# Two-layer hybrid encoder on one core: opening the next pair of heads while the one in front is still worked on, and moving attention's late products

## The chip, the cores and the metric

The kernel runs on one core of one Trainium2 chip, in one launch. The metric is the device time of that launch in microseconds (us). Five instruction queues matter: TensorE (PE, matrix products; its weight loads are listed apart as PEld), VectorE (DVE), ScalarE (ACT), GpSimd (POOL) and SyncE (SP), which issues most of the transfers. Every engine works through its own list of instructions in order, so an instruction that waits holds up all that stand behind it on that engine.

## The reference, cut to what matters

Each of two layers normalises the residual stream (1024 tokens by 1024 features), projects it with one matrix, feeds three kinds of heads, gates and projects their outputs and adds them to the stream; a norm of its own ends the program.

```python
def reference(x, positions, ...):
    for layer in range(DEPTH):                       # 2 layers
        h = rms_norm(x, norm_g[layer])
        cols = split_columns(h @ w_in[layer])
        y_gdn = gdn_branch(cols, ...)                # 6 heads, gated delta rule, both directions
        y_mla = mla_branch(cols, positions, ...)     # 6 heads, softmax attention with low-rank q and kv, rope
        y_rwkv = rwkv7_branch(cols, ...)             # 4 heads, RWKV-7 time mixing, both directions
        mix = jnp.concatenate([y_gdn.astype(F32), y_mla.astype(F32), y_rwkv.astype(F32)], axis=-1)
        mix = mix * jax.nn.silu(cols['gate'].astype(F32))
        x = x + mix.astype(x.dtype) @ w_out[layer]
    return rms_norm(x, final_norm_g)
```

The two recurrent kinds run a scan over the tokens, forwards and backwards. The GDN scan is written in chunks (a triangular solve inside each chunk, a state carried from chunk to chunk), and the kernel treats RWKV-7 in the same way.

## The kernel before, in words

**Two streams of work.** While the program is written out, a planner in Python decides the order of everything. One stream is the *scan stream*: first phase R (RWKV, 2 pairs of heads), then phase G (GDN, 3 pairs). Every pair is *opened* (its features loaded, normalised, transposed), its chunks are *prepared* (the products inside a chunk and the triangular inverse, L922 to L988), *stepped* through (16 steps that carry the state) and *closed* (both directions joined, transposed back by L839, gated into `mix`). The other is the *dense stream*: the input projection (27 tiles of 128 output columns), then the attention heads (MLA, 3 pairs by 2 halves of the tokens), into which the output projection of the RWKV heads (`out_part`) and the loading of output weights (`out_open`) are woven. What remains of the output projection comes after both.

**The rounds.** `chain` runs the scan stream in rounds. A round takes one piece from the scan thread and one from each preparation that is under way, and after each of them lets the dense stream advance by a share of `DENSE_R` or `DENSE_G`, in the planner's own microseconds. The dense generators yield such numbers after each group of instructions; `yield 0.0` gives way to the woven partner without counting, and `yield PAUSE` ends the dense stream's turn. The opening of a new pair is part of the first preparation of that pair (`nxt % nst == 0`); in the kernel before it starts only when no other preparation is under way, and `rwkv_open` waits besides (`GATE`) until the pair in front has delivered its `mix`. A scheduler then places the instructions on the engines, and `order()` ties the dense products on TensorE behind scan rows so that the two streams stay mixed as planned.

**The input projection** (`in_tiles`). A tile's weights arrive in `wf` (one buffer). `in_fetch` has two halves: the load and the column maximum `wc` on DVE (L529, L530); then a product with ones on TensorE that finds the maximum over partitions (`col_sum`, L509), a scale (DVE L510, L533, L534), and the split into two halves of f16, `wh` (ACT L537, L538) and `wl` (POOL L539). A tile has 48 products of 512 columns: for each of two halves of the tokens and eight blocks of the features the three products L378 to L380. The second half of the next tile's fetch is written into the middle of the present tile's products. `norm_T` normalises and transposes the input ahead of the first tile (64 transposes, L486). The evictions of the two halves (`post`) hand the tile on: a short convolution, a token shift, a gate, or the MLA latents (stored to DRAM).

**Attention** (`mla`). `latents` loads what the projection stored, squares it on ACT (L1512), sums over partitions by products with ones (L1523 to L1525), makes a reciprocal root on DVE (L397) and broadcasts it (L1544). `mla_q` projects the queries; their rotary part needs two more products (L1699, L1700), a combination on DVE (L1708) and a transfer that puts it beside the rest (L1715, `mq<-mr`). `mla_max` finds each query's maximum in a first pass of the scores (L1734, DVE L1735, L1739, transposed by L1744, moved by L1747 into `mnr`), `mla_main` computes scores (L1767 to L1769), exponentials (ACT L1771) and products with the values (L1778), `mla_side` is woven into it and holds the next queries and maxima, and `mla_tail` (L1810, two transfers through DRAM, L1824, L1829) normalises and gates.

**Scales of GDN** (`gdn_scales`). After the last gate column is projected, a chain of DVE and ACT work makes the decay factors; its products on TensorE begin with L795.

Of the kernel before, what the change touches and what calls it, by code (L numbers as in the profile page):

```python
# [222 lines left out]
DENSE_R = 0.85  # L223
DENSE_G = 1.05
LEAD = 4
GATE = "gate"
PAUSE = -1.0
# [6 lines left out]
class K:  # L234
# [307 lines left out]
    def in_tiles(self, l, tiles, xt, ss):  # L542
# [4 lines left out]
        w = next(f)  # L547
        yield from self.norm_T(l, xt, ss)
        hi, lo = self.h
        for i, (t, post, after) in enumerate(tiles):  # L550
# [4 lines left out]
            for nh in range(2):  # L555
                ps = self.A()
                sl = slice(512 * nh, 512 * nh + 512)
                for k in range(8):
                    ks = slice(128 * k, 128 * k + 128)
                    self.mm3(ps, [(wh[:, ks], wl[:, ks], hi[k][:, sl], lo[k][:, sl])], k == 0, k == 7)  # L560
                    yield 0.65
                    if nh and k == 2:
                        self.flush()
                    if not nh and k == 6 and i + 1 < len(tiles):
                        w = next(f)
                self.pending = post(nh, ps, sl, us) or self.pending
                yield 0.0
            if after:
                self.flush()
                after()  # L570
# [12 lines left out]
    def layer(self, l, xt, ss, last):  # L583
# [9 lines left out]
        with self.phase("R", 6, "right"):  # L593
            self.rwkv()
# [3 lines left out]
        with self.phase("G", 4, "right"):  # L598
            self.gdn()
# [10 lines left out]
    def dense_work(self, l, xt, ss):  # L610
# [16 lines left out]
        def scales():  # L627
            self.gdn_scales()

# [4 lines left out]
        for hp in range(3):  # L634
            tiles += [(8 + 3 * hp + j, self.conv_tile(hp, j), scales if hp == j == 2 else None) for j in range(3)]
# [124 lines left out]
    def gdn_scales(self):  # L760
# [31 lines left out]
        rows = scr[:, 528:784]  # L792
        ps = self.E()
# [367 lines left out]
    def chain(self, units, nst, ahead, early, stagger, dense, prep, step, close):  # L1161
# [48 lines left out]
        while S or ps or nxt < total:  # L1210
            if nxt < total and nxt <= done[0] + 1 + span and (not ps or ((nxt % nst or early) and len(ps) < span and ps[-1].at >= stagger)):
                ps.append(thread(preparation, nxt, nxt % 2))
                nxt += 1
# [34 lines left out]
    def rwkv_open(self, hp, w2):  # L1248
        nc = self.nc
        s = {"hp": hp, "w2": w2}  # L1250
        while hp and 5 + hp not in self.mix:
            yield GATE
# [192 lines left out]
    def rwkv_close(self, s):  # L1445
# [20 lines left out]
        sq = self.S("ysq")  # L1466
# [25 lines left out]
    def latents(self):  # L1492
# [9 lines left out]
        for nh in range(2):  # L1502
# [45 lines left out]

            for a in ((0, cq0, self.par("qg0"), 128, *c0), (0, t2, self.par("qg1"), 64, c1[0:64], c1[64:128]),
# [16 lines left out]
    def mla(self):  # L1566
# [3 lines left out]
        for pr, nh in units:  # L1570
            if pr == nh == 0:
                yield from self.weave(self.mla_first(), self.out_part(self.l))
# [33 lines left out]
    def mla_side(self, pr, nh):  # L1606
        if nh == 0:
            if pr == 0:
                yield from self.mla_q(pr, 1)
                for _ in range(4):  # L1610
                    yield 0.0
# [245 lines left out]
    def out_part(self, l):  # L1857
# [9 lines left out]
        for _ in range(6):  # L1867
            yield 0.0
# [106 lines left out]
```

## Time and profile before

| what | us |
|---|---|
| median of 3 runs | 2594.94 (2589.27 to 2595.14) |
| the profiled execution | 2594.93 |
| its span (first to last instruction) | 2593.1 |
| TensorE busy | 2274.3 (88%) |
| VectorE / ScalarE / GpSimd busy | 1681.8 / 1384.2 / 835.0 |
| granted TensorE clock, mean | 0.937 |

The stages of the first layer, from the timeline: the norm and its transposes up to 48, the first tiles of the projection alone up to 95, phase R from 95 to 600 (the steps of its two pairs from 150 to 312 and from 396 to 557), phase G from 600 to 1224 (steps of its three pairs from 617 to 792, 839 to 1009 and 1055 to 1222), the rest of the output projection up to 1307. The second layer repeats them: phase R from 1380 to 1880, phase G to 2500, output to 2593.

How to read the views that follow. A row of the waits gives the engine and line that waited, after the arrow what released it, then total us, how often, and the longest. A row of the windows gives a stretch of the span in us, its length, the busy time of TensorE (and, where more engines are listed, PE, PEld, DVE, ACT and POOL in this order), the mean granted clock as a share of full speed, the busy share of the DMA engines and GB/s. A row of the timeline gives the start, the duration, engine and line, output and inputs, and in brackets the idle time just before with its releaser. Durations of products on TensorE overlap, since they are pipelined.

### The profile page before, as it was taken

What the parts mean: (1) busy time and instruction counts of PE and PEld (TensorE: products, weight loads), DVE (VectorE), ACT (ScalarE), POOL (GpSimd) and SP (SyncE); (2) the same over time, 40 slices, a digit from 0 to 9 for tenths busy, and PEclk for the clock granted to TensorE, in tenths of its full rate; (3) what the DMA queues carried; (4) which work ended last, traced back from release to release, by engine and by line L of the source; (5) the groups of instructions that cost most, each with busy time, mean ns of one, the idle gap of its engine ahead of it and who ended that gap; (6) DMA issues with size and microseconds to landing.
All of it is one profiled execution on the core that took longest, in us unless ns stands there. A gap on an engine that the chain in (4) does not pass through costs nothing. (4 is left out here: it accounts for less than half of the span.)

```text
span 2593.1 us, 54912 instructions
## 1 busy us (share of the span) xinstructions
PE 2274.3 (88%) x21524; PEld 1391.3 (54%) x21524; DVE 1681.8 (65%) x3706; ACT 1384.2 (53%) x3077; POOL 835.0 (32%) x1079
## 2 busy tenths in 40 slices
PE   5999988898799889897989999898997998898978
PEld 3456555555565445554755555555555644455456
DVE  6566668845577775666245676777465777657655
ACT  5566656656445544554245665666463455455541
POOL 1223222323224535353012332232332256353510
PEclk9999999899889989898999989998997999898979
DMA  3122222223341111102212221222323411111131
GB/s 123 46 53 57 67 70 54 70 82 99 107 152 32 36 50 36 30 23 83 82 69 54 57 61 61 70 62 52 116 71 120 129 42 38 36 38 33 50 106 65
DMA packets 140338, 174.09 MB, mean 67 GB/s; under 512 B 37072, under 2 KB 95536, under 8 KB 140080
## 3 DMA queue, kind: packets, MB, share of 16 engines
q1 hardware_dynamic: 139936, 170.19, 21.7%
q8 instruction: 170, 2.79, 0.4%
q14 instruction: 88, 0.72, 0.1%
q0 software_dynamic: 144, 0.39, 0.1%
HBM read 106.88 MB, written 39.04 MB: 56 GB/s over the span
## 5 line engine op out<-in xcount | busy, mean ns | idle before, releaser
L378 PE MATMUL pa<-h,wh 128*128 128x512 f16 x864 | 335.1, 388 | 0.0
L379 PE MATMUL pa<-h,wh 128*128 128x512 f16 x864 | 334.3, 387 | 0.0
L380 PE MATMUL pa<-h,wl 128*128 128x512 f16 x864 | 333.3, 386 | 0.0
L948 DVE TENSOR_TENSOR z<-pb,c 128x256 f16<-128x256 f32 (+1 forms) x320 | 155.9, 487 | 149.5 <-PE pb L922 138.0
L926 ACT COPY bdz<-z 64x256 f16<-64x256 f16 (+1 forms) x384 | 172.8, 455 | 136.7 <-DVE z L948 112.2
L1773 POOL TENSOR_TENSOR md<-md,mp 128x512 f32<-128x512 f32 x144 | 188.5, 1313 | 133.3 <-ACT mp L1771 126.2
L539 POOL TENSOR_TENSOR wl<-wf,wh 128x512 f16<-128x512 f32 x108 | 127.6, 1196 | 282.6 <-ACT wh L538 274.9
L1778 PE MATMUL pa<-mp,mv 128*64 128x512 f32 x384 | 190.2, 634 | 0.0
L966 ACT CAST xT<-pe 128x512 f16<-128x512 f32 x256 | 150.8, 589 | 50.2 <-PE pe L965 49.3
L953 ACT CAST x<-pb 128x256 f16<-128x256 f32 (+1 forms) x320 | 134.8, 421 | 59.1 <-PE pb L922 58.0
L1735 DVE TENSOR_REDUCE mmx<-pa 128x1 f32<-128x512 f32 x192 | 131.3, 688 | 49.6 <-PE pa L1734 47.0
L1771 ACT ACTIVATE mp<-pa 128x512 f32<-128x512 f32 x192 | 114.5, 597 | 89.1 <-PE pa L1769 86.1
L927 DVE COPY bdz<-z 64x256 f16<-64x256 f16 (+1 forms) x384 | 150.5, 399 | 13.4 <-PE pe L958 0.9
L922 PEld LDWEIGHTS <-xT 128*128 128x128 f16 x1600 | 77.7, 99 | 106.3 <-issue 61.4
L1413 POOL TENSOR_TENSOR rs_e<-rs_z,rw_em 64x128 f32<-64x128 f32 x120 | 56.0, 482 | 239.6 <-DVE rs_z L1440 201.1
L922 PEld LDWEIGHTS <-bdgh 128*128 128x128 f16 x1920 | 89.3, 100 | 81.4 <-issue 43.5
L380 PEld LDWEIGHTS <-wl 128*128 128x128 f16 x864 | 85.6, 99 | 80.0 <-issue 8.3
L922 PE MATMUL pb<-z,xT 128*128 128x64 f16 x1600 | 108.9, 196 | 21.9 <-DVE z L948 20.0
L736 DVE SCALAR_TENSOR_TENSOR cacc<-raw,dv,cacc 128x512 f32<-128x512 f32 x144 | 120.5, 853 | 11.2 <-ACT cacc L730 9.5
L378 PEld LDWEIGHTS <-wh 128*128 128x128 f16 x864 | 90.1, 104 | 67.7 <-issue 9.6
L1734 PE MATMUL pa<-mk,mq 96*128 96x512 f32 (+1 forms) x192 | 93.4, 490 | 31.8 <-DMA mq<-mr 21.7
L379 PEld LDWEIGHTS <-wh 128*128 128x128 f16 x864 | 85.6, 99 | 57.8 <-issue 8.0
(462 smaller groups left out, 5683.1 us busy)
## 6 DMA issues: line engine op xcount, KB each, us to landing
wf<-in_w_in_dram SPq DMA_DIRECT2D x54, 512.0 KB
q_d<-cacc SPq DMA_DIRECT2D x18, 512.0 KB
rw_ka<-rw_kr SPq DMA_DIRECT2D x32, 256.0 KB
rw_ka<-rw_ak SPq DMA_DIRECT2D x64, 128.0 KB
gate_d<-gate SPq DMA_DIRECT2D x16, 512.0 KB
wof<-in_w_out_dram SPq DMA_DIRECT2D x16, 512.0 KB
xp_d<-mp SPq DMA_DIRECT2D x32, 256.0 KB
xo<-xp_d SPq DMA_DIRECT2D x16, 512.0 KB
```

Of the source, the lines that this page charges most:

```text
L378: self.did = nc.tensor.matmul(out, lhsT=lh, rhs=rh, start=(first and idx == 0), stop=False)
L379: self.did = nc.tensor.matmul(out, lhsT=lh, rhs=rl, start=False, stop=False)
L380: self.did = nc.tensor.matmul(out, lhsT=ll, rhs=rh, start=False, stop=(last and idx == n - 1))
L922: self.did = nc.tensor.matmul(ps[:, 64 * u:64 * u + 64], lhsT=st(lhsT, u), rhs=rhs(u), start=True, stop=True)
L926: nc.scalar.copy(zb[self.H[0], :, 0], t[self.H[0]])
L927: nc.vector.tensor_copy(zb[self.H[1], :, 1], t[self.H[1]])
L948: nc.vector.tensor_tensor(out=self.q8(z), in0=v(ps), in1=self.m8(self.c2(f"w{k}"), w), op=ALU.mult)
L953: nc.scalar.copy(f2(x), p1[:, :64 * nu])
L966: nc.scalar.copy(xn[:, g:g + 4].rearrange("p u h i -> p (u h i)"), p2)
L1735: nc.vector.tensor_reduce(out=mx[:, h, t:t + 1], in_=ps, axis=AX.X, op=ALU.max)
L1773: nc.gpsimd.tensor_tensor(out=acc[h], in0=prev[h] if t == 1 else acc[h], in1=pT, op=ALU.add)
L1778: self.did = nc.tensor.matmul(po[NR[h]], lhsT=vv[:, t, 2 * pr + h], rhs=pT[h], start=(t == 0), stop=(t == 7))
```

## The change

- The condition in `chain` loses its special case: a preparation that opens a new pair may start while the last preparation of the pair in front is under way. `rwkv_open` no longer waits for the `mix` of the pair in front. The phases get two more slots of scratch (6 to 8 and 4 to 6), and `rwkv_close` uses the tile `pbn` again in place of a slot of its own.
- `DENSE_R` goes from 0.85 to 1.0 and `DENSE_G` from 1.05 to 1.03.
- The second half of a fetch is written later: for the first tile after the ninth step of `norm_T` (before: ahead of all of it), for the others after the first group of the tile's second half (before: after the seventh group of its first half, ahead of that half's eviction).
- `gdn_scales` becomes a generator of the dense stream and pauses it for six turns ahead of L795.
- `latents` yields twice more ahead of its sums, in each half; at the start of attention both woven streams issue their first loads, and then pause for six turns.
- `mla_side` gives way eight times ahead of the second half's maxima, for each pair (before: four times, and for pair 0 only); `out_part` gives way once in place of six times.
- The scratch for descriptors of dynamic transfers becomes 8192 bytes.

```diff
-DENSE_R = 0.85
-DENSE_G = 1.05
+DENSE_R = 1.0
+DENSE_G = 1.03
...
         f = self.in_fetch(l, tiles[0][0])
         next(f)
-        w = next(f)
-        yield from self.norm_T(l, xt, ss)
+        for n, us in enumerate(self.norm_T(l, xt, ss)):
+            yield us
+            if n == 8:
+                w = next(f)
...
-                    if not nh and k == 6 and i + 1 < len(tiles):
+                    if nh and k == 0 and i + 1 < len(tiles):
                         w = next(f)
...
             if after:
                 self.flush()
-                after()
+                yield from after()
...
-        with self.phase("R", 6, "right"):
+        with self.phase("R", 8, "right"):
...
-        with self.phase("G", 4, "right"):
+        with self.phase("G", 6, "right"):
...
         rows = scr[:, 528:784]
+        for _ in range(6):
+            yield PAUSE
         ps = self.E()
...
-            if nxt < total and nxt <= done[0] + 1 + span and (not ps or ((nxt % nst or early) and len(ps) < span and ps[-1].at >= stagger)):
+            if nxt < total and nxt <= done[0] + 1 + span and (not ps or (len(ps) < span and ps[-1].at >= stagger)):
...
         s = {"hp": hp, "w2": w2}
-        while hp and 5 + hp not in self.mix:
-            yield GATE
...
-        sq = self.S("ysq")
+        sq = pbn
...
+            for _ in range(2):
+                yield 0.1
             for a in ((0, cq0, self.par("qg0"), 128, *c0), (0, t2, self.par("qg1"), 64, c1[0:64], c1[64:128]),
...
             if pr == nh == 0:
-                yield from self.weave(self.mla_first(), self.out_part(self.l))
+                first, part = self.mla_first(), self.out_part(self.l)
+                for g in (first, part):
+                    next(g)
+                for _ in range(6):
+                    yield PAUSE
+                yield from self.weave(first, part)
...
             if pr == 0:
                 yield from self.mla_q(pr, 1)
-                for _ in range(4):
-                    yield 0.0
+            for _ in range(8):
+                yield 0.0
             yield from self.mla_max(pr, 1)
...
-        for _ in range(6):
-            yield 0.0
+        yield 0.0
...
-    nc = _bacc.Bacc("TRN2", target_bir_lowering=False, num_devices=1)
+    nc = _bacc.Bacc("TRN2", target_bir_lowering=False, num_devices=1, dynamic_dma_scratch_size=8192)
```

Line numbers in the changed kernel differ by a few: one less up to the scales, one more in `chain`, the scans and their preparation (L839 becomes L840, L922 becomes L923), one less in the closing of RWKV and the latents, six more in attention (L1700 becomes L1706, L1734 becomes L1740, L1767 becomes L1773). How the change moves the rows of TensorE is seen at three places; a row has the line, the operation, output and inputs with their running numbers, and the width of the output.

TensorE at the first half of the latents in layer 0, where L1523 (in the changed kernel L1522) sums the squares in `mk`. Before, the rows just ahead are the scan's preparation:

```order
L958 LDWEIGHTS bdz_977_6574
L958 MATMUL pe_8005<-xs_1233_7908,bdz_977_6574 128x64
L1523 MATMUL pa_8021<-cst,mk_7962 128x1
L1524 MATMUL pa_8021<-cst,mk_7964 128x1
L1525 MATMUL pa_8021<-cst,mk_7966 128x1
```

and now:

```order
L978 LDWEIGHTS bdgl_979_6600
L978 MATMUL pb_8032<-x_1272_8014,bdgl_979_6600 128x64
L1522 MATMUL pa_8045<-cst,mk_7904 128x1
L378 MATMUL pa_8086<-wo_7920,mx_7910 128x512
L1523 MATMUL pa_8045<-cst,mk_7906 128x1
L379 MATMUL pa_8086<-wo_7921,mx_7910 128x512
L1524 MATMUL pa_8045<-cst,mk_7908 128x1
```

Products of `out_part` (`mx`, `wo`) now stand between the sums, and from the last product of the projection to the first sum there are 97 rows where there were 41.

TensorE at the second half's maxima of pair 1 in layer 0: the rotary products (L1699, L1700) end the queries, and the first L1734 with `mq_11370` is the first of these maxima; the earlier L1734 rows belong to the maxima of another half. Before, 44 rows lie from L1700 to it, the last of them the scan's outputs:

```order
L1699 MATMUL pa_11464<-c_7936,mw_1830_10387 128x512
L1700 MATMUL pa_11464<-c_7936,mw_1831_10388 128x512
L1734 MATMUL pa_11474<-mk_11226,mq_10401 128x512
...
L1128 MATMUL pc_11376<-gs_s_11442,gd_qg_10854 64x64
L1129 MATMUL pc_11376<-gs_u_11526,gd_pt_10873 64x64
L1734 MATMUL pa_11584<-mk_10841,mq_11370 128x512
```

and now 173:

```order
L1705 MATMUL pa_11614<-c_7878,mw_1861_10536 128x512
L1706 MATMUL pa_11614<-c_7878,mw_1862_10537 128x512
L1740 MATMUL pa_11624<-mk_11342,mq_10550 128x512
...
L923 LDWEIGHTS bdgh_978_6598
L923 MATMUL pb_11907<-i_79,bdgh_978_6598 128x64
L1740 MATMUL pa_11913<-mk_10982,mq_11531 128x512
```

Scan rows and the main part of attention have come in between.

TensorE at the end of layer 0: L1128 and L1129 (now L1129 and L1130) are the scan's last output products, L839 (now L840) transposes the closed pair, L378 with `mx` begins the rest of the output projection. Before:

```order
L1128 MATMUL pc_15085<-gs_s_15105,gd_qg_14708 64x64
L1129 MATMUL pc_15085<-gs_u_15126,gd_pt_14727 64x64
L839 MATMUL pe_15161<-cst,osum_12527 64x64 x16
L839 MATMUL pe_15179<-cst,osum_12527 64x64 x16
L378 MATMUL pa_15265<-mq_14357,mx_15224 128x512
```

and now:

```order
L1130 MATMUL pc_15026<-gs_u_15083,gd_pt_14573 64x64
L1775 MATMUL pa_15103<-mq_13537,mk_13384 128x512
L1784 MATMUL pa_14599<-mp_15048,mv_9164 64x512
L1784 MATMUL pa_14599<-mp_15069,mv_9164 64x512
L1784 MATMUL pa_14599<-mp_15091,mv_9164 64x512
L1784 MATMUL pa_14599<-mp_15107,mv_9164 64x512
L1816 MATMUL pa_15138<-md_14600,cst 64x512
L1816 MATMUL pa_15138<-md_14601,cst 64x512
L509 MATMUL pa_15203<-ngs_15201,cst 128x1
L840 MATMUL pe_15159<-cst,osum_12304 64x64 x16
L840 MATMUL pe_15177<-cst,osum_12304 64x64 x16
L378 MATMUL pa_15263<-mq_14690,mx_15222 128x512
```

The last products of attention stand behind the scan's last row, where before they stood ahead of it.

More of the change, by code (lines that the diff above doesn't have):

```diff
@@ L625, in plain @@
             return post
-        def scales():
-            self.gdn_scales()
         self.projected, self.pending = False, None
@@ L634, in dense_work @@
         for hp in range(3):
-            tiles += [(8 + 3 * hp + j, self.conv_tile(hp, j), scales if hp == j == 2 else None) for j in range(3)]
+            tiles += [(8 + 3 * hp + j, self.conv_tile(hp, j), self.gdn_scales if hp == j == 2 else None) for j in range(3)]
             if hp == 0:
```

## The prediction, made before the changed kernel ran

> **What bounds the kernel now.** The page's head and clock strip come first:
>
> ```profile
> span 2593.1 us, 54912 instructions
> PE 2274.3 (88%) x21524; PEld 1391.3 (54%) x21524; DVE 1681.8 (65%) x3706; ACT 1384.2 (53%) x3077; POOL 835.0 (32%) x1079
> PEclk9999999899889989898999989998997999898979
> ```
>
> TensorE works 88% of the span and the next engine 65%, and most slices are at or near full clock. Its busy time is no floor, though: several slices show 7 to 9 tenths of the clock, so some of the 2274.3 us is slow work. Next, who TensorE waited for (total, times, longest):
>
> ```profile
> PE pa L1734 <- DMA mq<-mr: 21.7, 4, 6.7
> PE pa L509 <- DVE wc L530: 20.0, 10, 5.0
> PE pe L958 <- DVE bdz L927: 20.0, 15, 2.4
> PE pa L1523 <- ACT mk L1512: 15.5, 2, 7.8
> PE pe L839 <- DVE osum L1152: 13.8, 2, 6.9
> PE pa L1544 <- DVE rq_y L397: 13.2, 4, 3.9
> PE pa L795 <- DVE scr L789: 7.2, 2, 3.6
> PE pa L1767 <- DMA mq<-mnr: 4.4, 6, 1.0
> ```
>
> Except for the many small waits of L958 (inside the scans), these are a few places per layer, each struck once or twice per layer. So I looked at each place by windows (length, PE busy, granted clock):
>
> ```profile
> core 0: us, PE busy (x), PEclk, DMA share, GB/s
> 502.00:513.00 11.00, 5.49 (x51) 0.53 0.14 24
> 676.00:697.00 21.00, 11.78 (x72) 0.51 0.48 152
> 710.00:728.00 18.00, 13.46 (x111) 0.53 0.30 95
> 935.00:953.00 18.00, 9.63 (x69) 0.53 0.32 103
> 1079.00:1100.00 21.00, 14.28 (x111) 0.51 0.12 33
> 1219.00:1243.00 24.00, 13.52 (x139) 0.50 0.23 68
> 1785.00:1797.00 12.00, 6.24 (x55) 0.57 0.13 22
> 1956.00:1977.00 21.00, 11.39 (x70) 0.51 0.50 154
> 1990.00:2008.00 18.00, 13.47 (x110) 0.53 0.29 97
> 2215.00:2233.00 18.00, 9.45 (x61) 0.53 0.33 101
> 2362.00:2377.00 15.00, 9.62 (x71) 0.54 0.11 28
> 2492.00:2517.00 25.00, 12.58 (x140) 0.52 0.23 62
> sum 222.00, PE 130.91; mean PE 10.91
> ```
>
> Six places, twice (layer 0, then layer 1): L795; the latents' first half; their second; the maxima of pair 1 (L1734); those of pair 2; the layer's end. Around each wait the clock stands near half, so a window costs its idle time and slow work besides. I take what a window could do at full clock as busy times clock (502 to 513: 5.49 x 0.53 = 2.9) and call the rest its loss (8.1). Over both layers the losses are 16.5 (L795), 30.2 and 21.8 (latents), 25.9 and 23.5 (maxima), 35.7 (end): 153.6 us, the **ceiling** of what these places can return. Of it 222.0 - 130.9 = 91.1 is plain idleness.
>
> **The change part by part.** The order of TensorE tells what now stands ahead of each late product; lengths are the trace's means for the same kinds of row, so each distance is an estimate.
>
> *Maxima.* What is late there:
>
> ```profile
> 739.07 0.50 PE L1700 MATMUL pa<-c,mw 64*128 64x512 f32 x1
> 743.33 2.52 SPq L1715 DMA_DIRECT2D mq<-mr  x4
> 940.14 0.68 DVE L1708 TENSOR_TENSOR mr<-pa,mr 64x512 f32<-64x512 f32 x1
> 945.11 2.48 SPq L1715 DMA_DIRECT2D mq<-mr  x4
> 949.08 0.76 PE L1734 MATMUL pa<-mk,mq 96*128 96x512 f32 x1 [6.67 <-DMA mq<-mr]
> ```
>
> From the rope product to the issue takes 4.3 us where nothing is in the way (739.07 to 743.33), from issue to use 4.0 (945.11 to 949.08): 8.3 us of chain, here lengthened by DVE reaching L1708 only at 940.14. In the order before some 4.9 us of TensorE work stands between; with eight turns given away there are 173 rows, some 18 us. Both pairs' waits (6.7 at the longest) should vanish: -20 of 25.9 for pair 1 and -15 of 23.5 for pair 2, whose window holds other small gaps.
>
> *Latents.* L1523 waits 7.8 us for a chain that begins with the store of the last projected half and ends in L1512. Between that half's last product and L1523 41 rows become 97, among them six 128x512 products of the output part, some 4.4 us against 0.5. So 3.9 of 7.8 us is covered, half of 30.2: -15. The second half's L1544 has 6 to 7 us of work behind its statistics instead of 1 to 3, against waits of 3.9 at most: -14 of 21.8.
>
> *GDN scales (L795).* Six pauses let scan rows pass: 9.3 us of work behind the last gate becomes 11.4. The wait was 3.6, so 2.1 of it goes, over half of 16.5: -9. The pauses add no work.
>
> *Layer's end.* The scan now ends ahead of attention's last products, and behind its last row stand one L1775, four L1784 and two L1816. By the means of the same rows before (0.43, 0.634 and 0.616 us) that is 4.2 us under a wait of 6.9. But TensorE also has less work between the last L1816 and the first use of mix[5], 13 us instead of 19, and the chain between them runs through transfers that were first issued at
>
> ```profile
> 1213.48 1.15 SPq L1817 DMA_DIRECT2D mrc<-md  x2
> ```
>
> and ended with mix[5] near 1226, 13 us. Taking 1 to 3 us of new wait against it, about half of 35.7 stays: -17.
>
> These sum to **-90** of 153.6.
>
> *First tile's weights.*
>
> ```profile
> 1312.62 0.59 PE L509 MATMUL pa<-wc,cst 128*128 128x1 f32 x2 [5.05 <-DVE wc L530]
> 57.67 37.12 SPq L526 DMA_DIRECT2D wf<-in_w_in_dram  x4
> 64.36 0.15 DVE L530 TENSOR_TENSOR wc<-wc 128x1 f32<-128x1 f32 x1
> 64.66 0.35 PE L509 MATMUL pa<-wc,cst 128*128 128x1 f32 x2 [1.31 <-DVE wc L530]
> ```
>
> L509 now stands behind 35 transposes (L486) that need nothing of it, so 5 us of waiting are filled in each layer: -9. The second to fourth tiles gain nothing: wf has one buffer, the next load goes out only at 57.67, once wl of the tile before is done, wc is ready at 64.36 and L509 follows. That ring takes 12 us a tile wherever L509 is put, and the 10.4 us of a tile's products hide in it.
>
> *Later tiles' weights.* L509 also moves behind the eviction between the two halves of a tile, two groups of three products. It shortens the lead of wl over its use by
>
> ```profile
> 439.56 0.38 PE L379 MATMUL pa<-h,wh 128*128 128x512 f16 x1
> 440.21 0.38 PE L379 MATMUL pa<-h,wh 128*128 128x512 f16 x1
> ```
>
> 0.65 us a group, 1.3 in all, and 2.8 with the scan rows woven in. Taking, tile by tile, the end of its second subtraction in this group of the page's list against its first product:
>
> ```profile
> L539 POOL TENSOR_TENSOR wl<-wf,wh 128x512 f16<-128x512 f32 x108 | 127.6, 1196 | 282.6 <-ACT wh L538 274.9
> ```
>
> of the 54 tiles most had wl ready 4 to 9 us early; eight in the scan stages had less than 2.8. (From L509 to that end takes 5 us unhindered and up to 20 in the scans.) If each of the eight loses 2.8 us it is 22, of which the next tile's lead returns a part: **+12** (bounds 0 and +60, all 46 scan-stage tiles losing 1.3 us).
>
> *Two pairs at once, denser dense work.* Opening pair 1 of RWKV while pair 0 is worked on moves its preparation 23 us forward; the step from pair 0's last to pair 1's first falls from 69 to 36 us of TensorE work, between GDN pairs from 40 to 27. Nothing is added; the gain is idleness only:
>
> ```profile
> 100.00:600.00 500.00, 456.13 (x4763) 272.22 (x4762) 341.89 (x744) 306.23 (x662) 146.56 (x187) 0.96 0.24 67
> ```
>
> TensorE idles 43.9 us in this R stretch, DVE (third count) 158. Some 4 us a layer in R and 2 at the two GDN seams: **-12**, bounds -40 (half of R's idleness) and +40 (DVE's share from 68% up at the denser turns, two preparations and a scan queued on it).
>
> *New waits.* The first maxima of pair 0 now come 6 us after their rope product, not 24, under the same 8.3 us chain: at least 2.3 us, 5 with the clock, in each layer: +10. The mnr chain before L1767 has a little less cover (it cost 4.4): +4. Two slots more, the reused kms and the smaller scratch (the trace has one transfer on POOL's queue, at the start) cost nothing that I see; the slots hide behind memory that nothing else used, and if the scratch delayed that one load, layer 0's start would pay for it once.
>
> Sum: -90 - 9 + 12 - 12 + 10 + 4 = -85. The profiled execution took 2594.93 us, its span 2593.1 with 1.8 around it, and the median is 2594.94: **2510 us**, -3.3%.
>
> **The clock.** About 62 of the 153.6 (130.9 busy less 68.4 at full rate) is slow work rather than idleness. A rule of the Trainium skill ("TensorE: Matmul & The Clock Gate", Part 1: The HAM clock gate) speaks against counting it: for modelling, the ramp costs under 1% of a typical span, here under 26 us. The windows above, half clock for 18 us at a stretch, already show more than that, so here the trace disagrees, and my sum goes by the windows. By the rule the sum would hold at most the idleness, which is the first rival.
>
> **The rivals.**
>
> *Only idleness returns.* The half-clock stretches stay, as they follow from the scans' thin rows and not from the waits. For: L958's 15 small waits remain under them. Against: every named wait has its own dip. Then -90 x 91.1/153.6 = -53, and 2594.9 - 53 - 9 + 12 - 12 + 14 = **2547**. The skill's rule above ends here.
>
> *The waits move.* The latents' chain begins with a transfer from the last projection, which moves too; L1512 is then as late as before (15 + 14 lost), mix[5] takes the end's gain (17), maxima of pair 0 wait twice the 5: -85 + 46 + 10 = -29, **2566**. For: one chain is exchanged for another in three places. Against: TensorE has other rows there in the order.
>
> *Two pairs give nothing or a little loss*, since DVE holds both: -12 becomes +12, **2534**.
>
> *Slower: late weights.* Every scan-stage tile waits for wl: DVE and ACT serve two preparations and a scan ahead of L510 and L537, and one wf buffer passes a delay on to the next tile. From 97 / 46 = 2.1 us a tile on it eats everything else (-97 without weights); if each tile loses the whole 2.8 us lead, it is +129: 2595 - 97 + 129 = **2627**. For: eight tiles were within 2.8 us. Against: most had 4 to 9.
>
> *The change doesn't do what it says*: seams hardly shorter in time, waits kept by an unforeseen queue (SP's, where output weights are now issued sooner): **2595**.
>
> **How the numbers follow.** Forecast 0.46; only idleness 0.15; waits move 0.13; two pairs give nothing 0.07; slower 0.10; no effect 0.05; still more than forecast (most of the ceiling) 0.04. What a measurement of this kernel can tell from no change is about 0.3%, 8 us. So faster 0.85, same 0.05, slower 0.10. The forecast's own range is 2480 to 2540; with the rivals at 2547 and 2566 and the gain's bounds below (-40 for two pairs and more of the ceiling), 8 in 10 lie in 2450 to 2575.
>
> **What would show it.** Right: among TensorE's waits the rows for mq<-mr of pairs 1 and 2, L1152 and the wc row of 5.0 gone or under 2 us, L1512 near 4, a new mq<-mr wait of 2 to 5 us at pair 0; the clock above 0.95; spans of R and G shorter by some 10 and 30 us. Wrong: a wait of L379 or L380 for wl or wh in the scan stages, DVE above 75% in R, half-clock stretches at the same places without idleness, or a wait of the output products (L378) for mix[5] of 5 us and more.

## The result, and the profile after

The changed kernel takes 2507.57 us (median of 4 runs, 2498.42 to 2517.25) against 2593.12 for the kernel before in the same session: a ratio of 0.9669 with a 95% interval of 0.9645 to 0.9694, or 86 us less. The forecast was 2510.

The page of the changed kernel, head, engines and clock strip:

```profile
span 2505.7 us, 54928 instructions
PE 2274.3 (91%) x21524; PEld 1386.8 (55%) x21524; DVE 1643.2 (66%) x3706; ACT 1386.2 (55%) x3077; POOL 844.7 (34%) x1079
PEclk9999999899899989999999999998998899899999
```

TensorE's busy time is 2274.3 us in both traces. The span fell by 87.4 us, and so did TensorE's idle time, from 318.8 (2593.1 - 2274.3) to 231.4. That the busy times agree to the tenth is chance: executions of the changed kernel differ by 19 us with the granted clock (2498.42 us at 0.955, 2517.25 at 0.948), so by my estimate a busy time from one trace is good to some 10 us. Where the idle time went is read from windows with the same four borders in each layer of both kernels: start to the layer's first projected product, to the last one, to the first of the maxima of pair 0, to the end of the last transposes L839 (L840). First the kernel before, layer 0 and then layer 1:

```profile
0.00:48.20 48.20, 17.60 (x133) 1.00 0.48 154
48.20:671.70 623.50, 567.72 (x5693) 0.96 0.23 65
671.70:769.10 97.40, 78.96 (x742) 0.81 0.48 153
769.10:1235.90 466.80, 407.21 (x3914) 0.92 0.14 42
1235.90:1331.10 95.20, 87.66 (x420) 0.93 0.25 91
1331.10:1951.80 620.70, 564.58 (x5693) 0.97 0.23 65
1951.80:2049.00 97.20, 78.77 (x742) 0.81 0.48 153
2049.00:2511.60 462.60, 402.94 (x3912) 0.93 0.15 44
```

and the changed one:

```profile
0.00:45.80 45.80, 18.24 (x133) 1.00 0.51 162
45.80:658.40 612.60, 566.34 (x5649) 0.96 0.23 66
658.40:746.60 88.20, 81.05 (x771) 0.85 0.53 168
746.60:1188.90 442.30, 406.77 (x3932) 0.95 0.15 45
1188.90:1281.70 92.80, 84.78 (x420) 0.97 0.26 95
1281.70:1896.50 614.80, 563.62 (x5647) 0.97 0.23 65
1896.50:1985.70 89.20, 81.11 (x772) 0.83 0.52 166
1985.70:2423.20 437.50, 402.64 (x3927) 0.96 0.16 46
```

Length less busy time, both layers together: from 38.1 to 35.6 us in the rest of the output projection and the norm, 111.9 to 97.4 in the projection (with phase R), 36.9 to 15.2 at the latents, 119.3 to 70.4 in the rest of phase G. More than half of the gain (48.9 of 87.4) lies in that last stretch, 21.7 at the latents. From the first projected product to the last, the stretch is 10.9 and 5.9 us shorter (layer 0, layer 1), from there to the end of phase G 33.7 and 33.1, close to the signs that the prediction gave (some 10 and 30).

The waits of TensorE that answer to those of the prediction:

```profile
PE pa L1522 <- ACT mk L1511: 11.0, 2, 6.0
PE pa L1740 <- DVE mmx L1741: 10.0, 12, 1.7
PE pe L840 <- DVE osum L1153: 8.6, 2, 4.5
PE pe L959 <- DVE bdz L928: 7.4, 8, 1.3
PE pa L509 <- DVE wc L530: 6.9, 7, 2.0
PE pa L1750 <- DVE mnm L1745: 6.1, 8, 1.1
PE pa L1773 <- DMA mq<-mnr: 5.6, 6, 1.6
PE pa L380 <- POOL wl L539: 0.8, 2, 0.4
```

No wait for the rotary queries (mq<-mr) is left, where it was the largest; the one for the latents' second half (rq_y) is gone as well, and so is that for the scales. The squares' wait went from 15.5 to 11.0, the joined outputs' from 13.8 to 8.6, that of L509 for wc from 20.0 to 6.9. The many small ones of the scan (L958, now L959, for bdz) went from 20.0 to 7.4, though no edit is aimed at them. The second pair is not the reason by itself: the same wait is 7.2 and 8.2 in the two kernels without it (experiments 1 and 5) and 10.4 in the one that has it alone (8). Which edit does it stays open. Others grew: that of the RWKV products (L1349, now L1348, for rw_ak) from 7.7 to 12.0.

The clock around the places, by windows of the changed kernel (the latents' first half and second half, the rotary queries of pair 1 in both layers, the maxima of pair 2):

```profile
660.00:690.00 30.00, 24.26 (x198) 0.72 0.47 157
702.00:722.00 20.00, 20.00 (x178) 0.74 0.44 131
915.00:937.00 22.00, 17.90 (x104) 0.61 0.31 90
2155.00:2176.00 21.00, 16.75 (x101) 0.59 0.32 83
1072.00:1094.00 22.00, 18.09 (x141) 0.77 0.07 19
```

The waits that stood in these windows are gone or shorter, but the clock came back only in part. At the latents' second half TensorE has no idle time left and still 0.74. At pair 1 the trace has half clock for 17.1 us in layer 0 in both kernels, from 935.9 to 953.0 before and from 917.7 to 934.8 after. Before, it began 6.5 us ahead of the wait; after, it lies ahead of the maxima, which come at 943.0, and no pause of TensorE in it is longer than 1.0 us. At pair 2 it fell from 20.5 us (1079.3 to 1099.8) to 10.2 in two pieces, in layer 1 from 13.7 to 3.4. Over the whole span the time at half clock fell from 326 to 243 us, but TensorE's work within it only from 224.5 to 214.6: what left the slow stretches is mostly idleness.

### The profile page after: what moved, and what is told of

The parts are those of the page before. It is cut to its first block, busy times and chain, and to the rows that moved or that the text cites. A ratio compares the mean times of both kernels' runs of the same rounds, so it can differ in the third digit from the quotient of the medians.

```text
span 2505.7 us, 54928 instructions
## 1 busy us (share of the span) xinstructions
PE 2274.3 (91%) x21524; PEld 1386.8 (55%) x21524; DVE 1643.2 (66%) x3706; ACT 1386.2 (55%) x3077; POOL 844.7 (34%) x1079
## 4 chain that ended last, share of the span: by engine, by line
PE 56%; DVE 19%; ACT 8%; issue 6%; POOL 6%; DMA 5%; SPq 0%; POOLq 0%; ACTq 0%; DVEq 0%
PE pa L378 5%; PE pa L1784 5%; PE pa L379 5%; PE pa L380 5%; PE pb L923 4%; DMA wf<-in_w_in_dram 3%; PE pa L1740 3%; POOL wl L539 2%; PE pa L1773 2%; DVE cacc L735 2%; PE pe L840 2%; PE pe L1348 2%; PE pe L966 2%; PE pa L1774 1%; PE pc L1114 1%
## 5 line engine op out<-in xcount | busy, mean ns | idle before, releaser
L378 PE MATMUL pa<-h,wh 128*128 128x512 f16 x864 | 335.6, 388 | 1.4 <-DVE h L491 1.4
L380 PE MATMUL pa<-h,wl 128*128 128x512 f16 x864 | 333.7, 386 | 0.8 <-POOL wl L539 0.8
L379 PE MATMUL pa<-h,wh 128*128 128x512 f16 x864 | 334.5, 387 | 0.0
L928 DVE COPY bdz<-z 64x256 f16<-64x256 f16 (+1 forms) x384 | 139.0, 365 | 17.4 <-PE pe L966 5.7
L923 PEld LDWEIGHTS <-bdgh 128*128 128x128 f16 x1920 | 93.4, 100 | 88.8 <-issue 56.8
L923 PEld LDWEIGHTS <-xT 128*128 128x128 f16 x1600 | 77.5, 100 | 97.2 <-issue 55.8
L380 PEld LDWEIGHTS <-wl 128*128 128x128 f16 x864 | 85.2, 99 | 81.6 <-issue 6.0
L378 PEld LDWEIGHTS <-wh 128*128 128x128 f16 x864 | 91.0, 105 | 66.0 <-issue 11.4
L923 PE MATMUL pb<-z,xT 128*128 128x64 f16 x1600 | 109.3, 197 | 16.7 <-DVE z L949 12.7
L529 DVE TENSOR_REDUCE wc<-wf 128x1 f32<-128x512 f32 x108 | 71.7, 680 | 71.8 <-DMA wf<-in_w_in_dram 71.5
L379 PEld LDWEIGHTS <-wh 128*128 128x128 f16 x864 | 85.3, 99 | 60.1 <-issue 8.4
```

The lines of the kernel that those rows point to most:

```text
L378: self.did = nc.tensor.matmul(out, lhsT=lh, rhs=rh, start=(first and idx == 0), stop=False)
L379: self.did = nc.tensor.matmul(out, lhsT=lh, rhs=rl, start=False, stop=False)
L380: self.did = nc.tensor.matmul(out, lhsT=ll, rhs=rh, start=False, stop=(last and idx == n - 1))
L923: self.did = nc.tensor.matmul(ps[:, 64 * u:64 * u + 64], lhsT=st(lhsT, u), rhs=rhs(u), start=True, stop=True)
L928: nc.vector.tensor_copy(zb[self.H[1], :, 1], t[self.H[1]])
```

## The experiments

Each kernel was timed beside the kernel before. A signed number of us behind a ratio is the ratio's distance from 1 applied to 2595 us, so the difference from the kernel before; the changed kernel stands at -86 by this measure. Theory A is the prediction's (each part pays for its own place); B and C say that two pairs at once are what fills TensorE. In the edits, a long condition is cut to its end, and `...` marks lines left out.

**1. The change without two pairs at once** (the rest kept):

```diff
-not ps or (len(ps) < span and ps[-1].at >= stagger)
+not ps or ((nxt % nst or early) and len(ps) < span and ps[-1].at >= stagger)
...
+        while hp and 5 + hp not in self.mix:
+            yield GATE
```

> The changed kernel with the old condition in the rounds and the old wait of the second RWKV pair for the first one's mix; all else as changed. Theory A (each part pays for its own place, the sum of the prediction): the two pairs at once are worth 12 us, so about 2520 us, and TensorE's waits for the maxima and the latents stay as short as in the changed kernel. Theory B (the overlap is what feeds TensorE; the moved products only follow from it): over 30 us are lost, 2538 or more, and some of the long waits come back. If two pairs at once give nothing, 2508 within 5.

Measured 2561.43 us, ratio 0.9856 (0.9835 to 0.9877), -37: 49 us of the gain are lost, the size that theory B has. Its other sign came in part only: no wait for the rotary queries is back and the squares' wait is shorter than in the changed kernel (7.6 against 11.0 us in all), while the joined outputs' is longer (13.4 against 8.6). The loss isn't idleness alone: in the profiled executions TensorE is idle for 259.3 us in place of 231.4, and busy for 2306.1 in place of 2274.3. The timeline shows a second reason for the loss. In layer 0 attention's last products and the scan's last step lie far apart:

```profile
1158.32 1.07 PE L1818 MATMUL pa<-md,cst 128*64 128x512 f32 x2
1203.37 0.42 PE L1130 MATMUL pc<-gs_u,gd_pt 64*64 64x64 f32 x2
```

and in the 44 us between them TensorE has the scan's rows only (windows of the same kernel):

```profile
1159.40:1203.80 44.40, 35.83 (x554) 0.75 0.11 26
```

The granted clock there is 0.75: these rows are slow as well. The densities 1.0 and 1.03 are thus too high for a scan without the overlap. Experiment 5 takes this apart.

**2. The change without the later maxima:**

```diff
             if pr == 0:
                 yield from self.mla_q(pr, 1)
-            for _ in range(8):
-                yield 0.0
+                for _ in range(4):
+                    yield 0.0
```

> The changed kernel with the old four turns given away for pair 0 only ahead of the second half's maxima (in place of eight for every pair). Theory A: the waits for the transfer of the rotary queries come back at pairs 1 and 2 in both layers, four of some 5 to 7 us; by the prediction's terms 35 us, 2543; if only idleness is at stake (the trace of the changed kernel still shows about half clock there, 0.61 and 0.59, so the clock was not won back) some 20 us, 2528. Theory B: with two pairs in work other rows fill these waits anyway, under 8 us, 2515 at most.

Measured 2509.41 us, ratio 0.9661 (0.9633 to 0.9689), -88: no difference, although two waits are back (waits of TensorE, total, times, longest):

```profile
PE pa L1740 <- ACT mq L409: 10.3, 2, 5.3
PE pa L1740 <- DVE gd_pt L1079: 7.0, 2, 4.0
```

Theory A asked for 20 to 35 us. Both stand right behind the transfer of the rotary queries, at pairs 1 and 2 in both layers. These are 17.3 us of waits that the time does not show. In the profiled run TensorE is idle for 241.1 us in place of 231.4, so about half of the waits did not even add idleness; its busy time is 2261.4 in place of 2274.3, a difference of the size by which executions differ.

**3. The change with attention's start as before:**

```diff
-            for _ in range(2):
-                yield 0.1
...
-                first, part = self.mla_first(), self.out_part(self.l)
-                for g in (first, part):
-                    next(g)
-                for _ in range(6):
-                    yield PAUSE
-                yield from self.weave(first, part)
+                yield from self.weave(self.mla_first(), self.out_part(self.l))
...
-        yield 0.0
+        for _ in range(6):
+            yield 0.0
```

> The changed kernel with attention's start as before: no two extra yields ahead of the latents' sums, no early first step of the two woven streams with six pauses, six turns given away in the output part. Theory A, prediction's terms: 29 us lost, 2537. Reading idleness alone in the changed trace (16.6 and 16.9 us around the latents before, 5.7 and 6.7 after): about 20 us, 2528, with a wait of over 7 us for the squares in both layers. Theory B: under 8 us.

Measured 2531.02 us, ratio 0.9741 (0.9723 to 0.9758), -67: 19 us are lost, the size that idleness alone gives (some 20; TensorE is idle for 254.8 us in place of 231.4). The waits it brings back:

```profile
PE pa L1522 <- ACT mk L1511: 19.2, 4, 9.4
PE pa L1543 <- DVE rq_y L397: 8.4, 4, 3.0
```

**4. The change with the fetch of the following tiles at its old place:**

```diff
-                    if nh and k == 0 and i + 1 < len(tiles):
+                    if not nh and k == 6 and i + 1 < len(tiles):
```

> The changed kernel with the second half of the fetch of the following tiles at its old place, in the middle of the tile's first half. Prediction's term: the late place costs 12 us, so this is faster, 2496. Rival: the changed trace shows hardly a wait for wl (0.8 us in all) and a shorter ring of the early tiles (10.9 us a tile in place of 12.0), so the old place costs some 3 us a layer there and more in the scans, and this is 5 to 12 us slower, 2513 to 2520.

Measured 2506.82 us, ratio 0.965 (0.9629 to 0.9671), -91: no difference. Neither the 12 us of the prediction nor the rival's loss is there. The old stall of L509 for wc is back in part, 14.5 us in ten waits where the changed kernel has 6.9.

In this kernel the projection took 6 us longer in layer 0 (47.2 to 665.9, against 45.8 to 658.4), and the rest of phase G 7 us less (751.4 to 1186.2, against 746.6 to 1188.9).

**5. The change without two pairs at once and with the old densities** (the edit of experiment 1, and `DENSE_R = 0.85`, `DENSE_G = 1.05`):

> The changed kernel without the two pairs at once and with the old densities 0.85 and 1.05; all other parts as changed. It tells whether the 50 us that the changed kernel lost without the overlap came from the overlap itself or from densities that no longer fit (the projection there ended 28 us earlier and the end of phase G was thin). Theory A (places add): two pairs and densities together are worth 12 us, 2520 to 2530. Theory C (the overlap itself feeds TensorE while attention waits): 2550 or more even with the old densities.

Measured 2528.26 us, ratio 0.974 (0.9724 to 0.9757), -67. Of the 49 us of experiment 1, 30 came from densities that no longer fitted. Overlap and densities together are worth 18 us on top of the other edits, near theory A's 12; all the other edits together 67, where the prediction's sum without the pair term was 73 (90 + 9 - 12 - 14). But that sum holds 17 for the layer's end, and in this kernel the wait there is what it was in the kernel before (6.9 us in each layer). With the end counted on the other side the forecasts are 56 and 29.

**6. The change with the old densities alone:**

> The changed kernel with the old densities 0.85 and 1.05, the overlap kept. Theory A: the densities only place the layer's end, about 2508 to 2520. Theory C: with two pairs in work the scans get through in fewer rounds, so the old densities leave dense work over at the end of phase G, and the tail after the last scan step grows: 2520 to 2540.

Measured 2544.98 us, ratio 0.982 (0.9799 to 0.984), -47: 39 us are lost, more than either theory has. Here the scan ends first, its last row at 1167.68 in layer 0, and attention goes on alone until 1208, waiting once for GpSimd's sum (timeline, then the window from the last L840 to the next layer's projection):

```profile
1167.68 0.33 PE L1130 MATMUL pc<-gs_u,gd_pt 64*64 64x64 f32 x4
1204.30 3.64 PE L1816 MATMUL pa<-md,cst 128*64 128x512 f32 x4 [4.99 <-POOL md L1779]
```

```profile
1180.30:1302.20 121.90, 106.91 (x487) 0.96 0.34 112
```

The changed kernel needs 92.8 us there.

**7. The kernel before with the later maxima alone** (the edit of experiment 2 the other way round):

> The kernel before with one edit: eight turns given away ahead of the second half's maxima for every pair. Theory A (the prediction's term): 35 us faster, ratio 0.9865. Idleness alone: the four waits of 5 to 7 us and nothing of the clock, some 20 us, 0.992. If the rows that stand ahead of the maxima now are only taken from later places (as without this edit the changed kernel was no slower): no change, 0.997 to 1.003.

Measured 2580.73 us, ratio 0.9946 (0.9929 to 0.9962), -14. On its own the edit pays, and less than the 21.7 us of its waits. They are gone, but another has grown to twice what it was; the row before, and then the row of this kernel:

```profile
PE pa L1744 <- DVE mnm L1739: 7.4, 8, 1.8
```

```profile
PE pa L1744 <- DVE mnm L1739: 15.0, 12, 2.8
```

The rows that now stand ahead of the maxima stood elsewhere, here between the maxima and the transposes of their result: at three of the six places in each layer, 8, 49 and 21 products of TensorE stood there before, and 0, 6 and 2 stand there now. In the profiled executions the idle time fell by 6.7 us (318.8 to 312.1) and the busy time by 11.2; the time at half clock around the maxima of pairs 1 and 2 fell in this kernel as well (in layer 0 from 37.6 us to 23.9). So whether a part of the -14 is clock and not idleness stays open.

**8. The kernel before with two pairs at once alone:**

```diff
-        with self.phase("R", 6, "right"):
+        with self.phase("R", 8, "right"):
...
-        with self.phase("G", 4, "right"):
+        with self.phase("G", 6, "right"):
...
-not ps or ((nxt % nst or early) and len(ps) < span and ps[-1].at >= stagger)
+not ps or (len(ps) < span and ps[-1].at >= stagger)
...
-        while hp and 5 + hp not in self.mix:
-            yield GATE
...
-        sq = self.S("ysq")
+        sq = pbn
...
-    nc = _bacc.Bacc("TRN2", target_bir_lowering=False, num_devices=1)
+    nc = _bacc.Bacc("TRN2", target_bir_lowering=False, num_devices=1, dynamic_dma_scratch_size=8192)
```

> The kernel before with the two pairs at once alone: the condition in the rounds, no wait of the second RWKV pair, the slots, the reused tile and the scratch that make room for it; densities, fetches, scales, latents and maxima as before. Theory A: 12 us faster, 0.995. Theory C: 30 to 50 us faster, 0.981 to 0.988, with the waits for the maxima shorter or gone although nothing was moved there.

Measured 2546.32 us, ratio 0.9815 (0.9796 to 0.9834), -48, theory C's size and four times the prediction's term. The slots, the reused tile and the scratch go with it, as room for the second pair. The wait for the rotary queries fell to about a third (21.7 before) although nothing was moved there, as theory C has it, and the scales' wait more than doubled (7.2 before):

```profile
PE pa L1732 <- DMA mq<-mr: 7.8, 2, 3.9
PE pa L795 <- DVE scr L789: 16.1, 2, 8.0
```

What the overlap does is seen at the layer's end in layer 0, by the last rows of attention (L1810) and of the scan (L1129). The kernel before:

```profile
1211.76 1.07 PE L1810 MATMUL pa<-md,cst 128*64 128x512 f32 x2
1223.77 0.42 PE L1129 MATMUL pc<-gs_u,gd_pt 64*64 64x64 f32 x2
```

and with two pairs at once (the same rows are L1808 and L1129):

```profile
1171.21 0.28 PE L1129 MATMUL pc<-gs_u,gd_pt 64*64 64x64 f32 x2
1206.98 1.97 PE L1808 MATMUL pa<-md,cst 128*64 128x512 f32 x2 [0.59 <-POOL md L1771]
```

The scan ends 53 us sooner, attention 4. Before, the layer's end hung on the scan; now it hangs on attention.

The two ends in layer 0 (us, end of the last such row), for the kernels that change them:

| kernel | scan | attention | time, from the kernel before |
|---|---|---|---|
| before | 1224 | 1213 | 0 |
| overlap alone (8) | 1171 | 1209 | -48 |
| all but overlap and densities (5) | 1186 | 1174 | -67 |
| all but the overlap (1) | 1204 | 1159 | -37 |
| all but the densities (6) | 1168 | 1208 | -47 |
| changed | 1176 | 1180 | -86 |
| changed, with a denser phase G (12) | 1197 | 1192 | -59 |

The best of them is one in which both streams end together. Where they end 40 and 44 us apart (6 and 1) the time is 39 and 49 us above the changed kernel's. But ends that meet are not enough, as the last row shows (experiment 12).

**9. The change without the pauses ahead of the scales** (`range(6)` becomes `range(0)` ahead of L796):

> The changed kernel without the six pauses ahead of the transposes of GDN's scales. Prediction's term: 9 us lost (the wait of 3.6 us in each layer and the clock around it), 2517. Idleness alone: 7 us. If the covered waits only move, as the maxima's did: no change, 2505 to 2511.

Measured 2503.09 us, ratio 0.9642 (0.9617 to 0.9666), -93: no difference from the changed kernel. Nor is the wait back: in this trace TensorE is not idle ahead of L796 in either layer. So the pauses are not what covers the scales in the changed kernel; which edit does is not shown.

**10. The change with the first tile's maximum ahead of the transposes:**

```diff
-        for n, us in enumerate(self.norm_T(l, xt, ss)):
-            yield us
-            if n == 8:
-                w = next(f)
+        w = next(f)
+        yield from self.norm_T(l, xt, ss)
```

> The changed kernel with the first tile's column maximum ahead of all 64 transposes again. Prediction's term: 9 us lost, 2517, TensorE waiting about 5 us for wc at each layer's start. In the changed trace the norm's stage of layer 0 was shorter by 2.4 us only (first projected tile at 45.8 in place of 48.2), so by that reading 5 us in all. No change if the transposes then wait for DVE in its place.

Measured 2504.46 us, ratio 0.9643 (0.9615 to 0.9671), -93: no difference. The wait is back in the list,

```profile
PE pa L509 <- DVE wc L530: 15.6, 8, 5.0
```

and the first projected product comes at 48.4 in place of 45.8, but the 2.6 us are not in the time. (In the kernels that keep the changed start it comes between 45.8 and 47.6.)

**11. More rows ahead of the latents' first sums:**

```diff
-            yield 0.1
-            yield 0.1
+            for _ in range(2 if nh else 5):
+                yield 0.1
             yield 1.5
```

> The changed kernel with three more yields ahead of the first half's sums of the latents: in the order 24 products of the output part stand ahead of the first sum in place of 6. The changed kernel still waits 5 and 6 us there. If covering a wait with work that would have been done anyway pays its idleness, as without the latents' yields (19 us), then 10 us faster than the changed kernel, 2497, ratio to the kernel before 0.963. If these products are missed later, as with the maxima: no change, 0.967.

Measured 2510.93 us, ratio 0.9678 (0.9652 to 0.9703), -84: no gain. The 11.0 us of the squares' wait are gone from the list, and these have come or grown:

```profile
PE pa L1773 <- DMA mq<-mnr: 11.7, 6, 2.7
PE pe L840 <- DVE osum L1153: 10.7, 2, 6.3
PE pa L378 <- DVE mp L1883: 6.4, 2, 4.4
```

That is 5.6 to 11.7, 8.6 to 10.7 and 6.4 new, 14.6 in all: an output product now waits for the accumulation in front of it. But the wait of the maxima for mmx fell as well, from 10.0 to 2.9, and TensorE's idle time as a whole fell, from 231.4 to 225.5, while its busy time rose from 2274.3 to 2283.2. So the new waits by themselves do not explain why nothing was gained, and that stays open.

**12. The change with `DENSE_G = 1.06` in place of 1.03:**

> The changed kernel with DENSE_G 1.06 in place of 1.03. It tells how sharp the fit of the densities is: with the overlap, 0.85 and 1.05 cost 39 us, and without it 1.0 and 1.03 cost 33 us against 0.85 and 1.05. If the dense stream only has to end a little before the scan: within 5 us of the changed kernel. If any step off the fit costs: 10 us or more, with the wait for the last pair's joined outputs back at 7 us, since in the order one row stands ahead of its transposes in place of nine.

Measured 2536.32 us, ratio 0.9773 (0.9744 to 0.9801), -59: 27 us lost for three hundredths. The ends still lie within 5 us of each other (scan 1197, attention 1192), so that isn't the only thing that counts. The waits show that many distances were dealt anew:

```profile
PE pe L840 <- DVE osum L1153: 13.4, 2, 6.7
PE pa L1773 <- DMA mq<-mnr: 12.1, 4, 5.6
PE pa L1773 <- DVE mr L1715: 9.7, 2, 5.2
```

The first of these was expected, the second and third were not. In the profiled runs the rest of phase G is idle for 26 us more over both layers (46.3 and 50.3 us in place of 35.5 and 34.9). Which other rows the denser stream ran out of stays open.

None of these kernels is faster than the changed one by more than the intervals hold; the four that undo a small edit (2, 4, 9, 10) lie level with it. Apart from 1 and 6, which leave densities that do not fit, the undoings that cost something are those of the latents (19 us) and of overlap with densities (18). If these two add, the other 49 of the 86 us belong to no edit that a run takes back by itself, and no run takes the four small edits back together.

## Why the prediction was right, point by point

**The total** of -85 against -86 measured. Split as in experiment 5, with the layer's end on the side of overlap and densities: all the other edits -56 forecast and -67 measured; overlap, densities and end -29 forecast and -18 measured (against the changed kernel, two sessions, each ratio known to about 0.2 to 0.25%). That the total fits to 1 us is luck, as the terms below show.

**The ceiling and the clock.** The step that failed is that slow work around a wait comes back with the wait. At pair 1 the wait vanished and the half clock lasted as long as before; at pair 2 half of it or more went. Over the span the work done at half clock fell by 10 us only (224.5 to 214.6). Counted as the prediction counts (busy time times clock), some 5 us of slow work came back, an estimate, against the 37 that the sum held. The mean clock rose from 0.937 to 0.951 because idle time left the slow stretches, and what was gained is idleness, within the some 10 us to which one trace's busy time is good. On this point the first rival was right, and the prediction's own sign of being wrong, half-clock stretches at the same places without idleness, came true at pair 1 and at the latents' second half. The rule of the Trainium skill ("TensorE: Matmul & The Clock Gate", Part 1: The HAM clock gate) that the ramp costs under 1% of a span stands there in a passage on the first products of a kernel; the prediction took it for half clock in the middle of the span, which it does not price. The rival's 2547 was 39 us too high: it scaled the six places only, while waits of the scans that neither it nor the forecast counted fell too (L959 for bdz from 20.0 to 7.4, L923 for z from 20.0 to 12.7). These make 20 of the 39; the rest is not accounted for wait by wait.

**Maxima, -35.** The waits went as forecast and the edit's own worth did not follow: -14 on the kernel before, 0 in the changed one. What failed is the step from a covered wait to a gain. Covering moves rows from elsewhere: experiment 7 shows the place that they left, the transposes behind the maxima. That the places they come from are as short of rows in the changed kernel fits experiment 2, but no run shows it place by place.

**Latents, -29.** Mis-sized: 19 measured (experiment 3), 21.7 of idleness. The wait of 7.8 should have fallen to 3.9 and fell to 4.9 and 6.0; the second half's is gone.

**Scales, -9, first tile, -9.** The scales' wait should have fallen by 2.1 of 3.6 us in each layer and went altogether, but not through the pauses, as experiment 9 shows. The first tile's fell as forecast (20.0 to 6.9 with the early tiles). Undoing either edit costs nothing that the intervals can tell. The first projected product came 2.4 us sooner in layer 0, not 4.5.

**The ring of the early tiles.** The step said that the ring through the one buffer takes 12 us wherever L509 is put. In the changed kernel L509 comes at 51.6, 62.5 and 73.4, so 10.9 us a tile. What got shorter is the way from the end of wl to the next column maximum, which held more than the load: 5.5 us in place of 6.7 at the second tile (56.67 to 62.20, before 57.65 to 64.36). With the early place (experiment 4) it is 6.8 and the tiles are 12 us apart again, and yet the whole is no slower.

**Later tiles' weights, +12.** 0 by experiment 4. L380 waited 0.8 us in all. In 24 of the 54 tiles the second half of wl was ready less than 0.5 us ahead of the tile's first product, or after it, but L378 and L379 stand ahead of the first product that needs wl, and its first half is ready sooner.

**Two pairs at once, -12.** Right as the last step on top of the others (-18 with its densities), wrong as an account of what it does. The term counted idle seams in R and G; the runs show that the scan as a whole gets shorter (53 us by its last row, experiment 8), and that the densities must follow: without them the overlap loses 21 us on top of the other edits (experiment 6 against 5), without the overlap they lose 30 (1 against 5). The prediction had no price for either mismatch.

**Layer's end, -17.** The transposes' wait fell from 6.9 to 4.2 and 4.5 where 2.7 was expected. But this is not a place of its own: it is where the two streams meet, and without overlap and densities the wait is back at 6.9 (experiment 5).

**New waits, +14.** Hardly there. The first maxima of pair 0 came close behind their rope product, and the chain took, in the changed kernel,

```profile
738.71 0.49 PE L1706 MATMUL pa<-c,mw 64*128 64x512 f32 x1
743.26 2.52 SPq L1721 DMA_DIRECT2D mq<-mr  x4
746.63 0.19 PEld L1740 LDWEIGHTS pa<-mk,mq 96*128 96x128 f32 x1
```

7.9 us from 738.71 to 746.63, where 8.3 was estimated. The rows in between, 6 us by the forecast from mean durations, filled these 7.9 us in the trace, and no wait is recorded ahead of L1740. The chain of mnr cost 5.6 in place of 4.4. The new waits of 1 to 3 us for mix[5] did not come.

So the sum was right with errors that cancel: too much for the clock (some 37 of the 90, by the share 62/153.6), too much for single waits, nothing for the scans' many small waits and the meeting of the streams. Neither the rival of late weights nor that of waits that only move came true for the change as a whole; something like the second is seen in single edits, where one wait went and another grew (experiment 7).

## What to carry to other kernels

Where two streams are interleaved on one engine, see which of them ends last, and fit the rate at which they are mixed again whenever an edit lets one of them get through faster: here the two kernels whose streams ended 40 and 44 us apart for want of that were 39 and 49 us slower than the changed one. Ends that meet are not enough: three hundredths of that rate cost 27 us with the ends 5 us apart. A covered wait is worth its length only while the rows that cover it are not missed elsewhere: four edits could be undone one by one here and nothing was lost, so such edits want a price as a group, which no run here gives. What this change as a whole returned is idle time; do not add the slow clock around a wait without a run that shows it come back. The reverse does not hold: a scan that is left alone on the engine costs clock too (0.75 in experiment 1, where more than half of the loss in the profiled executions is busy time).

## What the runs showed that was not expected

The granted clock does not follow the named waits closely: at pair 1 the wait of 6.7 us went, and the clock of the window rose from 0.53 only to 0.61 and 0.59, with 17 us of half clock as before. The same edits are not additive by a wide margin: overlap alone -48, all the other edits but the densities -67, both together -47, and with the densities -86. And waits that sum to 17 us (experiment 2) or 9 us (experiment 10, L509) in the list of TensorE can come and go without any change in the time.
